# A pad that sets the distance of the normalised parts to the weights modulo 512 bytes, and decay matrices from plain broadcasts

## The chip, the core and the metric

The kernel runs on one core of one Trainium2 chip. The metric is the device time of one execution in microseconds (us): the median of three runs, and beside it one profiled execution whose trace all rows here come from. TensorE (PE) multiplies matrices, with a queue for loading weights beside it (PEld); VectorE (DVE) and ScalarE (ACT) work on whole tiles; GpSimd (POOL) and SyncE (SP) mostly issue transfers. The 16 DMA engines are shared by all queues.

## What is computed

Two layers of a hybrid backbone over 256 latent and 256 context tokens of width 1024, in float32. A layer has a SwiGLU half-step, a mixer, and a second half-step; each begins with a modulated RMS norm `n`. The mixer projects `n` once and runs two branches, of which this change touches the gated DeltaNet:

```
h += 1/2 * gate1 * SwiGLU(mod(RMSNorm(h)))
n  = mod(RMSNorm(h)); p = n @ W_in
  g = -exp(a_log) * softplus(p_ab + dt_bias);  g = cumsum(g) in a chunk
  decay = exp(where(i >= j, g_i - g_j, -inf))            # per token block, direction and head
  a_mat = (k beta) k^T * decay;  qk = q k^T * decay; ...
h += gate2 * (m @ W_out)
h += 1/2 * gate3 * SwiGLU(mod(RMSNorm(h)))
```

## The kernel before

**Products.** Every dense product is float32 split in two float32r parts: a weights tile of 1024 x 128 is loaded on SP's queue into `raw` (three buffers, 512 KB), ACT copies it to `whi` (L112) and DVE makes `wlo = raw - whi` (L113), three buffers each. `mm3` (L142) then makes three matmuls for each of the eight row blocks: whi x high part, whi x low part, wlo x high part of the activations. A projection is 24 matmuls of 512 columns (both token streams), or 2 x 24 of 256 where the streams are taken apart (`project_halves`, the first three columns of a stage), or 24 of 256 where only the latent stream is needed.

**Stages.** Six times `open_norm` allocates the pair `nh`, `nl` (each 8 x 512 floats a partition) on the right side of SBUF, and a stage of projections reads it: (1) the first half-step of layer 0, 44 projections, from 26 to 295 us in the profile; (2) its mixer, 65 projections, to 845; (3) its second half-step, 44, to 1328; (4) the first half-step of layer 1, 44, 1457 to 1709; (5) its mixer, mostly 256 columns, 1834 to 2139; (6) its last half-step, all 256 columns, 2315 to 2441. Between them stand the second products of the half-steps, which read `gh`, `gl`, and the mixer's others, which read `yh`, `yl`, `oh`, `ol`, `mh`, `ml`.

**Addresses.** In the built program every buffer of `whi` and `wlo` starts at 192 modulo 512 bytes, and each matmul's block of weights is 512 bytes wide, each row block of activations 2048. `nh` and `nl` start at 480 in all six stages, 288 behind the weights; so do `yh` and `yl`. `gh`, `gl`, `oh`, `ol`, `mh` and `ml` are at 192, distance 0.

**Decays.** `mixer` advances the generator of `decays` and `decay_matrices` by one step for each of its first projections. `decays` makes the cumulated log decays `gc` (tile `x` in the rows) and stores them as rows in DRAM (`grow`). `decay_matrices` fills R, two tiles of 2 directions x 2 blocks x 8 heads x 128 x 128. For each of the eight (stream, direction, block) it writes mask minus `gc` of its own position with DVE (L507), adds the row of all 128 positions by an accumulating transfer of 512 KB on POOL's queue (L511), and exponentiates 128x1024 on ACT (L513).

**Order.** The order on each engine is made by a scheduler when the program is built, from program order and priorities: the split of weights has high priority, and the depthwise conv (`cy`, L822 and L824, 8 x 31 taps a layer on DVE) fills in from the end of the decays. An engine runs its instructions in that order, so what stands behind a waiting one waits too.

Of the kernel before, what the change touches and what calls it, by code (L numbers as in the profile page):

```python
# [12 lines left out]
F32 = mybir.dt.float32  # L13
F32R = mybir.dt.float32r
AF = mybir.ActivationFunctionType
ALU = mybir.AluOpType
# [16 lines left out]
CP = (1000, 0)  # L33


def blk(b):
    return slice(32 * b, 32 * b + 32)

# [8 lines left out]
class Net:  # L47
# [3 lines left out]
    def __init__(self, ctx, tc, a, out):  # L51
        self.tc, self.nc, self.a, self.out = tc, tc.nc, a, out
        nc = tc.nc
        pool = lambda name, bufs, **kw: ctx.enter_context(tc.tile_pool(name=name, bufs=bufs, **kw))
        self.cp = pool("cp", 1)
        self.vp = pool("vp", 2)
        self.sp = pool("sp", 2)
        self.rawp = pool("rawp", 3)
        self.wp = pool("wp", 3)
        self.hp = pool("hp", 1)  # L60
        self.wk = pool("wk", 2)
        self.pm = pool("pm", 4, space=PSUM)
        self.px = pool("px", 4, space=PSUM)
        self.dp = pool("dp", 1, space=DRAM)
        self.beside([], 1)
        self.small = nc.sync
        cst = lambda name, n=128: self.cp.tile([128, n], F32, name=name)
        self.ident = cst("ident")
        make_identity(nc, self.ident)
        self.ones = cst("ones")  # L70
        nc.vector.memset(self.ones, 1.0)
        self.mhalf = cst("mhalf", 16)
        nc.vector.memset(self.mhalf, -0.5)
        self.tri = [cst("tri0"), cst("tri1")]
        make_upper_triangular(nc, self.tri[0])
        make_lower_triangular(nc, self.tri[1])
        self.cap = [cst("cap0"), cst("cap1")]
        for d in range(2):
            nc.vector.tensor_scalar(out=self.cap[d], in0=self.tri[d], scalar1=-1.0, scalar2=1e6, op0=ALU.add, op1=ALU.mult)
        self.sel = cst("sel", 63)  # L80
        nc.vector.memset(self.sel, 0.0)
        nc.vector.memset(self.sel[:, 31:32], 1.0)
# [274 lines left out]
    def open_norm(self):  # L357

        self.np_ctx = ExitStack()
        pool = self.np_ctx.enter_context(self.right("np"))  # L360
        self.n = (pool.tile([128, KT, T], F32R, name="nh"), pool.tile([128, KT, T], F32R, name="nl"))

    def norm(self, y, q, s, bc=None, ks=range(KT)):

        nc = self.nc
        nh, nl = self.n
        st = STREAM[s]
        bc = bc if bc is not None else self.rstd(self.acc[s], D)[:, :256]
        for k in ks:
            t1 = self.wk.tile([128, 256], F32, tag="t1", name="t1", bufs=3)  # L370
            nc.vector.scalar_tensor_tensor(out=t1, in0=self.h[:, k, st], scalar=y.nA[:, q, k, s:s + 1], in1=bc,  # L371
                                           op0=ALU.mult, op1=ALU.mult)
            B = y.mods[:, 3 * q, k, s:s + 1]
            nc.scalar.activation(out=nh[:, k, st], in_=t1, func=AF.Identity, bias=B)  # L374
            nc.vector.scalar_tensor_tensor(out=nl[:, k, st], in0=t1, scalar=B, in1=nh[:, k, st].bitcast(F32),  # L375
                                           op0=ALU.add, op1=ALU.subtract)
# [74 lines left out]
    def decays(self, y, ps):  # L451


        nc, sp = self.nc, self.sp
        flat = lambda x: x.rearrange("p d t h -> p (d t h)")
        ab = self.w512("ab")
        nc.vector.tensor_copy(out=ab[:32, :], in_=ps[:32, :])
        pt = self.psx()
        for t in range(4):
            nc.tensor.transpose(pt[:, t * 32:(t + 1) * 32], ab[:32, t * 128:(t + 1) * 128], self.ident[:32, :32])  # L460
        pv = pt[:, :128].rearrange("p (t x d h) -> p x d t h", t=4, x=2, d=2)
        x, g, e = self.cols("x"), self.cols("g"), self.cols("e")
        y.beta = self.cols("beta")
        nc.vector.tensor_tensor(out=x, in0=pv[:, 0], in1=self.dtb[:, y.l].unsqueeze(2).to_broadcast([128, 2, 4, 8]), op=ALU.add)
        for d in range(2):
            nc.scalar.activation(out=y.beta[:, d], in_=pv[:, 1, d], func=AF.Tanh, scale=0.5)
        nc.vector.tensor_scalar(out=flat(y.beta), in0=flat(y.beta), scalar1=0.5, scalar2=0.5, op0=ALU.mult, op1=ALU.add)

        nc.vector.scalar_tensor_tensor(out=flat(e), in0=flat(x), scalar=-1.0, in1=flat(x), op0=ALU.mult, op1=ALU.min)
        nc.scalar.activation(out=flat(e), in_=flat(e), func=AF.Exp)  # L470
        nc.scalar.activation(out=flat(e), in_=flat(e), func=AF.Ln, bias=self.ones[:, 0:1])
        nc.vector.scalar_tensor_tensor(out=flat(x), in0=flat(x), scalar=0.0, in1=flat(e), op0=ALU.max, op1=ALU.add)
        nc.vector.tensor_tensor(out=g, in0=x, in1=self.decay[:, y.l].unsqueeze(2).to_broadcast([128, 2, 4, 8]), op=ALU.mult)
        yield
        pg = self.psx()
        for d in range(2):
            nc.tensor.matmul(pg[:, d * 32:(d + 1) * 32], lhsT=self.tri[d], rhs=flat(g)[:, d * 32:(d + 1) * 32], start=True, stop=True)
        nc.tensor.matmul(pg[:, 64:128], lhsT=self.ones, rhs=flat(g), start=True, stop=True)
        y.gc = gc = x
        gl, y.egc, y.egl, y.kd = e, self.cols("egc"), self.cols("egl"), self.cols("kd")  # L480
        nc.vector.tensor_copy(out=flat(gc), in_=pg[:, :64])
        nc.vector.tensor_copy(out=flat(gl), in_=pg[:, 64:128])
        nc.scalar.activation(out=flat(y.egc), in_=flat(gc), func=AF.Exp)
        nc.scalar.activation(out=flat(y.egl), in_=flat(gl), func=AF.Exp)
        nc.vector.tensor_tensor(out=flat(gl), in0=flat(gl), in1=flat(gc), op=ALU.subtract)
        nc.scalar.activation(out=flat(y.kd), in_=flat(gl), func=AF.Exp)

        yield
        y.rows = []
        for j, v in enumerate((gc, y.egc)):  # L490
            ps = self.psx()
            nc.tensor.transpose(ps[:64, :128], flat(v), self.ident)
            sb = self.w512("gr")[:64, :128]
            nc.vector.tensor_copy(out=sb, in_=ps[:64, :128])
            dr = self.dp.tile([64, 128], F32, name=f"grow{y.l}{j}")
            nc.sync.dma_start(out=dr, in_=sb)
            y.rows.append(dr)

    def decay_matrices(self, y, R):

        nc = self.nc
        for s in range(2):
            for d in range(2):
                for tt in range(2):
                    t = 2 * s + tt
                    e = R[s][:, d, tt]
                    nc.vector.tensor_tensor(out=e, in0=self.cap[d].unsqueeze(1).to_broadcast([128, 8, 128]),  # L507
                                            in1=y.gc[:, d, t].unsqueeze(2).to_broadcast([128, 8, 128]), op=ALU.subtract)
                    r0 = d * 32 + t * 8
                    ev = e.rearrange("p h i -> p (h i)")  # L510
                    nc.gpsimd.dma_start(out=ev, in_=y.rows[0][r0:r0 + 8, :].rearrange("a b -> (a b)").partition_broadcast(128),  # L511
                                        accum_op=ALU.add)
                    nc.scalar.activation(out=ev, in_=ev, func=AF.Exp)  # L513
                    yield

    def inverse_norms(self, y, ss):
# [63 lines left out]
    def solve(self, y, R, pool):  # L580
# [8 lines left out]
        for s in range(2):  # L589
            for b in range(4):  # L590
                for d in range(2):
                    nc.scalar.activation(out=G[blk(b), d, s * 16:(s + 1) * 16, :],
                                         in_=R[s][blk(b), d, :, :, blk(b)].rearrange("p t h i -> p (t h) i"), func=AF.Copy)
# [23 lines left out]
    def merge_blocks(self, y, R, X, XT, pool, xpool, beside):  # L617
# [3 lines left out]
        XN = xpool.tile([128, 32, 64], F32, name="XN")  # L621
        XB = xpool.tile([128, 2, 32, 32], F32, name="XB")
        nc.gpsimd.memset(XN[blk(0), :, 32:], 0.0)
        nc.gpsimd.memset(XN[blk(3), :, :32], 0.0)
        for d in range(2):
# [510 lines left out]
```

## Time and profile before

| | us |
|---|---|
| median of 3 runs | 2510.61 (2509.51 to 2510.81) |
| profiled execution | 2517.16 |
| its span, first to last instruction | 2515.4 |
| PE busy in the span | 2410.1 (96%) |
| DVE busy | 1774.5 (71%) |
| ACT busy | 956.0 (38%) |

The three matmul groups on `nh` and `nl` and the three on `gh` and `gl` hold nearly all of PE's time. A matmul's duration in the trace runs from its start to the end of its results, so consecutive ones overlap, and their sum is more than the engine's busy time; what a matmul costs is the distance from its start to that of the next. PE's clock is at its full 2.4 GHz, shown as 1.0, but for short stretches behind idle time, where it is 0.5. The mixers hold the idle pieces: around 485 and 1890, where the decays are made, and later around the solve and the scan.

### The profile page before, as it was taken

How to read it: one execution, taken by the hardware profiler on the slowest of the kernel's cores; microseconds unless marked ns; L12 is line 12 of the kernel's file. 1: busy time of each engine (PE TensorE's matmuls, PEld its weight loads, DVE VectorE, ACT ScalarE, POOL GpSimd, SP SyncE). 2: the span in 40 equal slices, each digit the busy share in tenths (PEclk: the TensorE clock that was granted, in tenths of full speed). 3: DMA queues.
4: the chain of work that ended last, by engine and by line, in shares of the span. 5: the costliest groups of instructions: out<-in, count | busy, mean ns of one | idle time of the engine just before them, and what ended most of it. 6: DMA issues, size and time to landing. Idle time of an engine off the chain costs nothing. (4 is left out here: it accounts for less than half of the span.)

```text
span 2515.4 us, 38318 instructions
## 1 busy us (share of the span) xinstructions
PE 2410.1 (96%) x15099; PEld 2043.3 (81%) x15099; DVE 1774.5 (71%) x3023; ACT 956.0 (38%) x1578; POOL 51.7 (2%) x111
## 2 busy tenths in 40 slices
PE   7999999999999999999999999999988998978998
PEld 5777778787887887887777888778887886878998
DVE  4766777699999665576667564444468999966554
ACT  3222222435443643332222232222245556544443
POOL 0000000100000000000000000000010000000000
PEclk9999999999999999999999999999999999988999
DMA  8556665744644474455555544444466572355664
GB/s 253 165 164 175 173 176 172 170 133 113 207 137 118 145 224 151 116 156 158 163 157 160 152 126 126 126 125 133 120 173 178 169 218 79 108 174 164 198 184 138
DMA packets 566773, 394.61 MB, mean 157 GB/s; under 512 B 27704, under 2 KB 513218, under 8 KB 564930
## 3 DMA queue, kind: packets, MB, share of 16 engines
q1 hardware_dynamic: 555606, 371.33, 51.2%
q0 software_dynamic: 2304, 8.39, 1.7%
q10 hardware_dynamic: 8684, 12.45, 1.5%
q8 instruction: 118, 1.93, 0.3%
q14 instruction: 61, 0.50, 0.1%
HBM read 358.43 MB, written 33.69 MB: 156 GB/s over the span
## 5 line engine op out<-in xcount | busy, mean ns | idle before, releaser
L142 PE MATMUL pm<-nh,whi 128*128 128x512 f32 (+1 forms) x2544 | 907.8, 359 | 23.2 <-ACT whi L112 16.3
L142 PE MATMUL pm<-nh,wlo 128*128 128x512 f32 (+1 forms) x2544 | 903.3, 356 | 2.9 <-DVE wlo L113 2.2
L142 PE MATMUL pm<-nl,whi 128*128 128x512 f32 (+1 forms) x2544 | 903.3, 356 | 0.0
L112 ACT ACTIVATE whi<-raw 128x1024 fp32r<-128x1024 f32 (+1 forms) x450 | 469.1, 1044 | 1109.3 <-PE pm L142 857.7
L113 DVE TENSOR_TENSOR wlo<-raw,whi 128x1024 fp32r<-128x1024 f32 (+1 forms) x450 | 541.1, 1204 | 237.3 <-ACT whi L112 233.2
L142 PEld LDWEIGHTS pm<-nh,whi 128*128 128x128 f32 x2544 | 480.9, 190 | 115.1 <-ACT whi L112 25.1
L142 PEld LDWEIGHTS pm<-nh,wlo 128*128 128x128 f32 x2544 | 480.9, 189 | 79.2 <-DVE wlo L113 4.4
L142 PEld LDWEIGHTS pm<-nl,whi 128*128 128x128 f32 x2544 | 481.3, 190 | 73.6 <-DVE nl L375 1.0
L296 DVE SCALAR_TENSOR_TENSOR aacc<-adaw,sc,aacc 128x512 f32<-128x512 f32 x448 | 312.3, 747 | 164.8 <-DMA adaw<-ada_w_in 164.7
L824 DVE SCALAR_TENSOR_TENSOR cy<-cx,cdw,cy 128x512 f32<-128x512 f32 (+1 forms) x480 | 272.0, 612 | 1.3
L142 PE MATMUL pm<-gh,whi 128*128 128x512 f32 (+1 forms) x770 | 268.8, 349 | 1.7 <-DVE h L380 1.7
L142 PE MATMUL pm<-gl,whi 128*128 128x512 f32 (+1 forms) x770 | 267.4, 347 | 0.0
L142 PE MATMUL pm<-gh,wlo 128*128 128x512 f32 (+1 forms) x770 | 267.3, 347 | 0.0
L142 PEld LDWEIGHTS pm<-gh,whi 128*128 128x128 f32 x770 | 145.7, 189 | 26.4 <-issue 3.4
L142 PEld LDWEIGHTS pm<-gh,wlo 128*128 128x128 f32 x770 | 145.7, 189 | 18.9 <-issue 0.8
L142 PEld LDWEIGHTS pm<-gl,whi 128*128 128x128 f32 x770 | 145.7, 189 | 17.6
L428 DVE TENSOR_TENSOR silu<-silu,pm 128x512 f32<-128x512 f32 (+1 forms) x88 | 54.5, 619 | 77.3 <-PE pm L142 70.2
L380 DVE SCALAR_TENSOR_TENSOR h<-pm,gate,h 128x256 f32<-128x256 f32 x80 | 36.4, 480 | 63.3 <-PE pm L142 63.0
L112 ACT ACTIVATE gh<-silu 128x512 fp32r<-128x512 f32 (+1 forms) x88 | 50.5, 573 | 39.1 <-DVE silu L428 39.0
L374 ACT ACTIVATE nh<-t,mods 128x256 fp32r<-128x256 f32 x88 | 39.9, 502 | 61.1 <-DVE t L371 61.0
L113 DVE TENSOR_TENSOR gl<-silu,gh 128x512 fp32r<-128x512 f32 (+1 forms) x88 | 54.4, 618 | 0.0
L142 PE MATMUL pm<-mh,whi 128*128 128x256 f32 (+1 forms) x152 | 48.3, 320 | 2.2 <-ACT mh L112 2.2
(248 smaller groups left out, 2376.9 us busy)
## 6 DMA issues: line engine op xcount, KB each, us to landing
raw<-ffn_w_in SPq DMA_DIRECT2D x208, 512.0 KB, 4.1
adaw<-ada_w_in SPq DMA_DIRECT2D x144, 512.0 KB, 4.0
raw<-w_in_in SPq DMA_DIRECT2D x130, 512.0 KB, 4.2
raw<-ffn_w_in SPq DMA_DIRECT2D x64, 448.0 KB, 4.3
R<-grow POOLq DMA_DIRECT2D x16, 512.0 KB, 13.9
raw<-conv_proj_in SPq DMA_DIRECT2D x16, 512.0 KB, 6.5
raw<-dn_proj_in SPq DMA_DIRECT2D x16, 512.0 KB
raw<-w_out_in SPq DMA_DIRECT2D x16, 512.0 KB, 4.1
```

What stands on the lines that cost most here:

```text
L112: nc.scalar.activation(out=hi, in_=x, func=AF.Copy)
L113: nc.vector.tensor_tensor(out=lo, in0=x, in1=hi.bitcast(F32), op=ALU.subtract)
L142: nc.tensor.matmul(ps, lhsT=u[:, j, :], rhs=v[:, k, tok], start=k == 0 and p == 0, stop=k == n - 1 and p == 2)
L296: nc.vector.scalar_tensor_tensor(out=st.acc[:, s], in0=wt[:, j], scalar=c, in1=st.acc[:, s], op0=ALU.mult, op1=ALU.add)
L374: nc.scalar.activation(out=nh[:, k, st], in_=t1, func=AF.Identity, bias=B)
L380: self.nc.vector.scalar_tensor_tensor(out=self.h[:, m, st], in0=ps[:, st], scalar=y.gate[:, q, m, s:s + 1], in1=self.h[:, m, st], op0=ALU. ...
L428: nc.vector.tensor_tensor(out=t, in0=t, in1=pb[:, tok], op=ALU.mult)
L824: nc.vector.scalar_tensor_tensor(out=dst, in0=src, scalar=w, in1=dst, op0=ALU.mult, op1=ALU.add)
```

## The change

Two things are changed. `open_norm` allocates a third tile `home` behind the pair, used by nothing, whose size puts the pair at 0, 64, 256, 448, 288 and 288 bytes behind the weights modulo 512 in the six stages (starts at 192, 256, 448, 128, 480 and 480). And `decay_matrices` no longer accumulates: four plain broadcasts a layer of 1 MB each put the rows into R, DVE adds the mask, and the subtraction of `gc` moves into the exponential as its bias, one 128x128 instruction a head, with `ngc = -gc` made in `decays`.

```diff
+HOMES = (0, 64, 256, 448, 288, 288)
...
         self.n = (pool.tile([128, KT, T], F32R, name="nh"), pool.tile([128, KT, T], F32R, name="nl"))
+        pool.tile([128, ((288 - next(self.homes) - 32) % 512 + 32) // 4], F32, name="home")
...
             y.rows.append(dr)
+        y.ngc = self.cols("r")
+        nc.vector.tensor_scalar(out=flat(y.ngc), in0=flat(gc), scalar1=-1.0, scalar2=None, op0=ALU.mult)
 
     def decay_matrices(self, y, R):
...
+        for s in range(2):
+            for d in range(2):
+                r0 = d * 32 + s * 16
+                nc.gpsimd.dma_start(out=R[s][:, d].rearrange("p t h i -> p (t h i)"),
+                                    in_=y.rows[0][r0:r0 + 16, :].rearrange("a b -> (a b)").partition_broadcast(128))
         for s in range(2):
             for d in range(2):
                 for tt in range(2):
                     t = 2 * s + tt
                     e = R[s][:, d, tt]
-                    nc.vector.tensor_tensor(out=e, in0=self.cap[d].unsqueeze(1).to_broadcast([128, 8, 128]),
-                                            in1=y.gc[:, d, t].unsqueeze(2).to_broadcast([128, 8, 128]), op=ALU.subtract)
-                    r0 = d * 32 + t * 8
-                    ev = e.rearrange("p h i -> p (h i)")
-                    nc.gpsimd.dma_start(out=ev, in_=y.rows[0][r0:r0 + 8, :].rearrange("a b -> (a b)").partition_broadcast(128),
-                                        accum_op=ALU.add)
-                    nc.scalar.activation(out=ev, in_=ev, func=AF.Exp)
+                    nc.vector.tensor_tensor(out=e, in0=e, in1=self.cap[d].unsqueeze(1).to_broadcast([128, 8, 128]), op=ALU.add)
+                    for h in range(8):
+                        nc.scalar.activation(out=e[:, h], in_=e[:, h], func=AF.Exp, bias=y.ngc[:, d, t, h:h + 1])
                     yield
```

The scheduler orders the mixers anew; outside them the order stays. On DVE in the mixer of layer 0, from the first instruction on R (R_3394 and R_3395 are the two tiles, cap the masks, x is gc, cy the conv's taps), it was:

```order
L507 TENSOR_TENSOR R_3394<-cap_101,x 128x1024
L113 TENSOR_TENSOR wlo<-raw,whi 128x1024
L485 TENSOR_TENSOR e<-e,x 128x64
L507 TENSOR_TENSOR R_3394<-cap_101,x 128x1024
L507 TENSOR_TENSOR R_3394<-cap_102,x 128x1024 x2
L923 SCALAR_TENSOR_TENSOR glu<-glu,pm 128x512
L113 TENSOR_TENSOR wlo<-raw,whi 128x1024
L494 COPY gr<-px 64x128 x2
L507 TENSOR_TENSOR R_3395<-cap_101,x 128x1024 x2
L507 TENSOR_TENSOR R_3395<-cap_102,x 128x1024 x2
L113 TENSOR_TENSOR wlo<-raw,whi 128x1024
```

The same place in the changed kernel, from behind the copies of the rows (R_3396 and R_3397 are the two tiles):

```order
L833 SCALAR_TENSOR_TENSOR cy<-cx,cdw,cy 128x512 x5
L117 TENSOR_TENSOR wlo<-raw,whi 128x1024
L833 SCALAR_TENSOR_TENSOR cy<-cx,cdw,cy 128x512 x3
L831 TENSOR_SCALAR cy<-cx,cdw,v_209 128x512
L833 SCALAR_TENSOR_TENSOR cy<-cx,cdw,cy 128x512 x2
L520 TENSOR_TENSOR R_3396<-R_3396,cap_101 128x1024
L117 TENSOR_TENSOR wlo<-raw,whi 128x1024
L932 SCALAR_TENSOR_TENSOR glu<-glu,pm 128x512
L520 TENSOR_TENSOR R_3396<-R_3396,cap_101 128x1024
L520 TENSOR_TENSOR R_3396<-R_3396,cap_102 128x1024 x2
L117 TENSOR_TENSOR wlo<-raw,whi 128x1024
```

The eight instructions on R stood ahead of the transfers and now stand behind them, with taps of the conv and the copies of the rows (`gr`) ahead of them. On ACT in the mixer of layer 1, around the first exponentials (R_14856 is R's first tile), it was:

```order
L112 ACTIVATE whi<-raw 128x1024
L513 ACTIVATE R_14856<-R_14856 128x1024
L112 ACTIVATE whi<-raw 128x1024
L513 ACTIVATE R_14856<-R_14856 128x1024
L922 ACTIVATE glu<-pm 128x256
L513 ACTIVATE R_14856<-R_14856 128x1024
L112 ACTIVATE whi<-raw 128x1024
```

And in the changed kernel (R_14915 is that tile, r is ngc):

```order
L116 ACTIVATE whi<-raw 128x1024 x2
L931 ACTIVATE glu<-pm 128x256
L522 ACTIVATE R_14915<-R_14915,r 128x128 x6
L116 ACTIVATE whi<-raw 128x1024
L522 ACTIVATE R_14915<-R_14915,r 128x128 x7
L116 ACTIVATE whi<-raw 128x1024
L522 ACTIVATE R_14915<-R_14915,r 128x128 x6
```

One whi more stands ahead of the first exponential, and from there on five to seven exponentials of 128x128 stand between two whi, where one or two of 128x1024 stood.

## Rows read from the trace of the kernel before

**Rows 1.** The page's engines, and the span with the granted clock of TensorE.

```profile
PE 2410.1 (96%) x15099; PEld 2043.3 (81%) x15099; DVE 1774.5 (71%) x3023; ACT 956.0 (38%) x1578; POOL 51.7 (2%) x111
...
core 0: 2515.4 us, clock 0.984
```

**Rows 2.** Groups by shape: count, busy us, mean ns of one, idle before.

```profile
L142 PE MATMUL pm<-nl,whi 128*128 128x512 f32 x1632 | 647.0, 397 | 0.0
...
L142 PE MATMUL pm<-nl,whi 128*128 128x256 f32 x912 | 256.4, 284 | 0.0
...
L142 PE MATMUL pm<-gl,whi 128*128 128x512 f32 x462 | 180.3, 390 | 0.0
```

**Rows 3.** Line 142: count, ns min/median/max, first and last start; two stretches.

```profile
L142 PE MATMUL pm<-nl,whi x158: 393/395/397, 1584.8 to 1694.7; 128*128 128x512 f32 x158
...
L142 PE MATMUL pm<-gh,wlo x119: 389/389/389, 1714.7 to 1794.9; 128*128 128x512 f32 x119
```

**Rows 4.** The same at 256 columns, in three stretches.

```profile
L142 PE MATMUL pm<-nl,whi x315: 277/278/280, 2324.8 to 2434.7; 128*128 128x256 f32 x158
...
L142 PE MATMUL pm<-ml,whi x26: 283/283/283, 1050.8 to 1059.8; 128*128 128x256 f32 x26
...
L142 PE MATMUL pm<-yh,whi x40: 280/280/280, 2256.0 to 2269.7; 128*128 128x256 f32 x40
```

**Rows 5.** Stretches: width; busy (count) of PE, PEld, DVE, ACT, POOL; clock, DMA.

```profile
26.00:295.00 269.00, 266.08 (x1284) 206.93 (x1281) 186.52 (x286) 80.47 (x111) 0.00 (x0) 1.00 0.63 179
520.00:640.00 120.00, 119.70 (x522) 91.97 (x521) 119.54 (x167) 53.85 (x105) 1.36 (x16) 1.00 0.47 136
1070.00:1328.00 258.00, 256.21 (x1193) 204.79 (x1192) 175.92 (x264) 77.86 (x105) 1.07 (x1) 1.00 0.55 157
```

**Rows 6.** Stretches beside the decays of the two mixers.

```profile
463.00:498.00 35.00, 30.00 (x126) 22.89 (x124) 20.00 (x27) 14.65 (x16) 7.90 (x8) 0.99 0.91 198
498.00:501.00 3.00, 3.00 (x7) 2.42 (x8) 3.00 (x5) 1.06 (x2) 0.00 (x0) 0.51 0.59 150
1866.00:1900.40 34.40, 21.19 (x144) 20.08 (x142) 15.35 (x21) 14.25 (x16) 7.03 (x8) 0.80 1.00 214
1883.00:1887.00 4.00, 4.00 (x22) 3.94 (x21) 0.85 (x1) 1.99 (x2) 0.86 (x1) 0.57 1.07 215
1895.70:1900.40 4.70, 4.16 (x18) 3.87 (x18) 4.65 (x10) 4.70 (x7) 0.00 (x0) 0.50 0.67 171
```

**Rows 7.** Waits (us, times, longest) from 463 and from 1866; one row of PE's timeline.

```profile
ACT R L513 <- DMA R<-grow: 18.1, 6, 8.4
...
PE pm L142 <- ACT whi L112: 11.8, 2, 8.6
ACT whi L112 <- DMA raw<-w_in_in: 7.5, 1, 7.5
...
1881.51 0.39 PE L142 MATMUL pm<-nh,whi 128*128 128x256 f32 x1 [3.18 <-ACT whi L112]
```

**Rows 8.** DMA queues (packets, MB, share): from 468:493, 1874:1892, 930:936.

```profile
q0 software_dynamic: 1149, 4.19, 85.1%
...
q0 software_dynamic: 918, 3.37, 94.1%
q1 hardware_dynamic: 915, 0.47, 12.6%
...
q1 hardware_dynamic: 622, 2.39, 97.9%
```

**Rows 9.** Instructions on R, and others like the new exponentials, on DVE and ACT.

```profile
L507 DVE TENSOR_TENSOR R<-cap,x x16: 1206/1216/1219, 452.1 to 1882.6; 128x1024 f32<-128x1024 f32 x16
...
L112 ACT ACTIVATE whi<-raw 128x1024 fp32r<-128x1024 f32 x13 | 13.7, 1053 | 15.3 <-DMA raw<-w_in_in 7.5 <-PE pm L142 5.2 <-issue 2.5
L513 ACT ACTIVATE R<-R 128x1024 f32<-128x1024 f32 x8 | 8.3, 1054 | 12.0 <-DMA R<-grow 12.0
...
L878 ACT ACTIVATE osq<-o x48: 292/294/354, 881.8 to 2218.8; 128x128 f32<-128x128 f32 x48
```

More of the change, by code (lines that the diff above doesn't have):

```diff
@@ L66, in __init__ @@
         self.small = nc.sync
+        self.homes = iter(HOMES)
         cst = lambda name, n=128: self.cp.tile([128, n], F32, name=name)
```

## The prediction

> **What bounds the kernel now.** I read the page's engine line first [rows 1]: TensorE (PE) is busy 96% of the span at a mean granted clock of 0.984, so time goes where PE matmuls go, or where PE waits. The groups by shape come next [rows 2]: 1632 × 3 matmuls of 512 columns and 912 × 3 of 256 columns read nh or nl, 462 × 3 of 512 columns read gh or gl. Their mean durations (397, 390 ns) overlap and are no price; the price is the distance from one start to the next. For that I took stretches in which PE runs one shape without a break and divided first to last start by the count. In [rows 3], nl,whi x158 starts from 1584.8 to 1694.7: 109.9 us over 157 × 3 steps, as three groups alternate, is 233.3 ns a matmul. gh,wlo x119 from 1714.7 to 1794.9 is 80.2 over 118 × 3, 226.6 ns. Same shape, same weights tiles, same full clock. What differs is the address: nh and nl start 288 bytes behind the weights modulo 512, gh and gl at 0. At 256 columns it is the other way round [rows 4]: nl x315, 109.9 over 314 × 3, 116.7 ns; ml (distance 0) x26, 9.0 over 25 × 3, 120.0 ns. The durations say the same without a division: 389 ns at every matmul of gh against 393 to 397, 283 for ml against 277 to 280 for nl and 280 for yh, which also stands at 288. So the distance matters, by 6.7 ns one way and 3.3 the other.
>
> Here the Trainium skill speaks against the change. "TensorE: Matmul & The Clock Gate", section "Step-by-step: what each phase is for", says that PE has two independent SBUF read ports, so that loading the next weights doesn't steal read bandwidth from the running matmul. By that rule the pad would change nothing, and the sum would keep its second half alone. The two starts above disagree with it, and it is weighed as a rival below.
>
> Last I looked for PE's idle time. The largest single pieces lie where each mixer makes its decays [rows 6]: in 463 to 498 PE is busy 30.0 of 35.0, and the next 3.0 run at clock 0.51; in 1866 to 1900.4 PE is busy 21.19 of 34.4, and of that two pieces of 4.0 and 4.16 run at 0.57 and 0.50.
>
> **Part A, the pad.** It adds no instruction. Distances become 0, 64, 256, 448, 288, 288 in the order of the stages: first half-step of layer 0, its mixer, its second half-step, first half-step of layer 1, its mixer, last half-step. The last two stay as they are. Counts follow from the loops, 24 matmuls a projection:
> - Stage 1: 44 projections, 1056 matmuls of 512 columns, distance 0, the one row I have. About 1000 of them lie in unbroken runs: 1000 × 6.7 = 6.7 us.
> - Stages 3 and 4: 41 projections in 512 columns, 984 each, and 3 in halves, 144 of 256. With the price of distance 0 each gives 984 × 6.7 = 6.6, less 144 × 3.3 = 0.5: 6.1 us, together 12.2.
> - Stage 2: 62 projections, 1488 × 6.7 = 10.0, less 0.5. Here VectorE (DVE) is the cover that could run out: 119.54 of 120 us busy in 520 to 640 [rows 5], with the depthwise conv between the splits. The order of its instructions is fixed, so a PE that is 2.9% faster leads to a wait for wlo once the lead of three weight buffers is used up. DVE is busy only 20.00 of the 35 us beside the decays [rows 6], and gets some of that back. I take 7.5 us of the 9.5.
>
> In stages 1 and 3 DVE is busy 186.52 of 269 and 175.92 of 258 [rows 5], and stage 4 has stage 3's products, so nothing is late next there.
>
> No row shows 64, 256 or 448. The rows bound them by 0 (as at 288) and 6.7 ns (as at 0). 256 is only 32 from 288, which speaks for nothing; but 0, 64, 256 and 448 are whole multiples of 64 and 288 is not, and 64 and 448 are 64 from 0. I take 6.7 for all three and keep the ends. Below the lower end: a distance may also be as much worse than 288 as 0 is better, 240 ns. Above: 512 columns at 2.4 GHz are 213.3, 13.2 ns more than the row at 0 leaves.
> Sum of part A: 6.7 + 12.2 + 7.5 = 26.4 us; ends of it 6.7 and, with another 6.7 ns on 3456 matmuls, 49.
>
> **Part B, the decays.** Removed, per layer: 8 accumulating transfers of 512 KB on POOL's queue, 8 DVE subtractions of 1.22 us, 8 exponentials of 1.05 us [rows 9]. Added: 4 plain broadcasts of 1 MB, 8 DVE additions of the same shape (1.22, no difference), one 128x64 negation (a sixteenth of the columns), 64 exponentials of 128x128. What the old transfers cost is in [rows 8]: in layer 0 they move 4.19 MB in the 25 us from 468; in layer 1, from 1874 to 1892, they hold 94.1% of the 16 DMA engines and move 3.37 MB in 18 us, 187 GB/s, while the queue of the weights gets 0.47 MB, less than one 512 KB tile. That is what PE waits for [rows 7]: PE for whi 11.8 us, whi for raw 7.5, and [rows 9] the exponentials for their transfers 12.0, with whi behind them on ScalarE (ACT). Loss now: layer 0, 5.0 idle + 3.0 × 0.5 at half clock = 6.5; layer 1, 13.2 idle + 1.7 + 2.1 at half clock = 17.0.
>
> A plain transfer in large packets reaches 2.39 MB in 6 us, 400 GB/s [rows 8]; 4.19 MB take 10.5 us alone, some 12 beside the weights, against 25. In layer 1 the hold begins at 1866, and PE's first wait of more than a microsecond at 1878.3 (a start at 1881.51 after 3.18 idle, [rows 7]): PE went on for 12 us on what was in buffers. So the new hold ends about when PE runs dry; one tile must then land and be split, about 4 us of idle time, with one dip of the clock (1.7). In layer 0 a projection takes twice as long, the buffers last twice as long, and I leave 1 us.
>
> The new cost is on ACT. A 128x128 exponential lies between an eighth of the old one, 0.13, and the longest osq, 0.35 (a Square of 128x128, SBUF to SBUF) [rows 9]; it has osq's shape, so I take osq's 0.294. 64 × 0.294 = 18.8 us a layer against 8 × 1.05 = 8.4. The waiting instruction's followers are whi and glu on ACT: in layer 1 six exponentials (1.8) stand between two whi (1.05), 2.8 us and what glu takes, some 3.0 a projection where PE needs 24 × 0.1167 = 2.8. Over ten projections 2 us. New waits: the DVE addition waits for the broadcast, with wlo queued behind it; since the conv's taps and several wlo now stand ahead of the first addition, I price it at 0, at most the 8.4 us that ACT's longest wait for a transfer lasts now [rows 7]. Left after: layer 0 1, layer 1 4 + 1.7 + 2 = 7.7. Gain 5.5 + 9.3 = 14.8, taken as 15. Ends: 23.5 (all of it), and 0 (ACT's 2 × 10.4 us take it back).
>
> **Sum.** The profiled execution took 2517.2 us, 1.8 around its span of 2515.4. Less 26.4 and 15 it is 2475.8. The median of the runs is 2510.6, 6.6 below the profiled one; less 41.4 it is 2469.
>
> **The rivals.**
> - *Only some distances help.* One or more of 64, 256, 448 behaves as 288. For: 288 itself is an unlucky one, with 256 beside it. Losing stages 2 to 4 leaves 6.7 + 15 = 22: 2489. Chance 18%.
> - *The distances are better than 0.* Another 6.7 ns on 3456: 2469 − 20 = 2449. Nothing in the rows excludes it. Chance 13%.
> - *The pad does nothing:* nl and gl differ by something other than the address. Against: yh, in another tile, has durations like nl's, and ml, again in another, is slower than both [rows 4]. Only part B: 2510.6 − 15 = 2496. Chance 5%. This is also what the Trainium skill's rule above would lead to.
> - *The broadcasts do nothing.* Packets twice as large starve the weights as before, or ACT is the bound. Only part A: 2484. Chance 12%.
> - *The distances are worse: slower than before.* Place: stages 2 to 4, 3456 matmuls of 512 columns. At 240 ns they cost 23 us more, against 7 from stage 1, and with ACT's longer exponentials eating part B, 2510.6 + 16 = 2527. With part B kept it decides from 239.6 ns on average, (6.7 + 15) / 3456 = 6.3 above 233.3; with part B gone from 235.2. Chance 5%.
>
> **How the numbers follow.** The forecast, all four distances about like 0 and the decays mostly free, has the rest, 47%, and gives 2469 ± 14. The range goes from 2440 (better distances with most of the 23.5) to 2500 (part B alone, or half of both). About 0.2%, 5 us, is what a measurement can tell from no change: faster than 2505.6 has 91%, as the only cases that reach it are the last one and a failure of both parts (4%); slower 5%.
>
> **What would show it.** Right: the 512-column step in stage 1 falls to 226.6 and the durations to 389 throughout; the steps of stages 2 to 4 lie at or below that; the last two stages keep 116.7; in the decays' stretch of each mixer the software queue's hold falls from 25 to 12 us, PE's waits for whi from 11.8 to about 4. Wrong: steps of 233 or more at 64, 256 or 448; PE waiting for wlo from 520 to 800 with DVE full; ACT full between the exponentials with PE waiting for whi.

## The result, and the profile after

The changed kernel takes 2482.33 us in the median of four runs (2477.48 to 2488.85) beside 2510.45 us for the kernel before: a ratio of 0.989, 95% interval 0.9867 to 0.9913. The prediction was 2469 us, in a range of 2440 to 2500. The sign and the range held; 28 us came where 41.4 were forecast.

The page's engines and the span of the profiled execution after, which answer to [rows 1]:

```profile
PE 2391.7 (96%) x15099; PEld 2048.7 (82%) x15099; DVE 1775.8 (71%) x3025; ACT 976.6 (39%) x1690; POOL 41.0 (2%) x103
...
core 0: 2487.0 us, clock 0.983
```

TensorE (PE) is busy 18.4 us less, and ScalarE (ACT) 20.6 us more, which are the exponentials in pieces; VectorE (DVE) is where it was, 1775.8 for 1774.5. The gain is placed by the stages. The table gives each stage's length in us, from its first matmul on `nh` or `nl` to the first matmul of what follows (on `gh` behind the projections of a half-step, on `yh` in the mixer of layer 0, on `oh` in that of layer 1), for five profiled executions (the last three columns belong to experiments below):

| stage (distance after) | before | after | pad only | broadcasts only | best distances |
|---|---|---|---|---|---|
| 1, first half-step, layer 0 (0) | 268.0 | 262.1 | 262.2 | 266.7 | 261.2 |
| 2, mixer, layer 0 (64) | 453.0 | 441.5 | 449.8 | 446.7 | 441.1 |
| 3, second half-step, layer 0 (256) | 257.5 | 251.8 | 251.2 | 255.7 | 251.0 |
| 4, first half-step, layer 1 (448) | 252.1 | 251.7 | 251.7 | 252.0 | 246.0 |
| 5, mixer, layer 1 (288) | 389.1 | 385.4 | 388.0 | 383.3 | 381.4 |
| 6, last half-step (288) | 125.8 | 125.9 | 126.0 | 126.7 | 121.8 |

Stages 1 and 3 became 5.9 and 5.7 us shorter, close to the forecast (6.7 and 6.1). Stage 4 became 0.4 shorter where 6.1 were forecast. Single lengths are good to about 2 us: with the broadcasts alone, which leave stages 1 and 3 as they are, these are 1.3 and 1.8 us shorter. The steps say why. Line 146 of the kernel after is the line of [rows 3] (count, ns min/median/max of a duration, first and last start in us); one stretch each of stages 1 to 4, then the halves of stage 4 at 256 columns:

```profile
L146 PE MATMUL pm<-nh,whi x70: 387/390/396, 222.3 to 269.3; 128*128 128x512 f32 x70
...
L146 PE MATMUL pm<-nl,whi x144: 391/392/393, 450.7 to 548.9; 128*128 128x512 f32 x144
...
L146 PE MATMUL pm<-nh,whi x78: 387/389/396, 1181.8 to 1234.2; 128*128 128x512 f32 x78
...
L146 PE MATMUL pm<-nh,whi x166: 392/396/399, 1554.8 to 1670.3; 128*128 128x512 f32 x166
...
L146 PE MATMUL pm<-nh,whi x32: 275/276/367, 1440.0 to 1450.6; 128*128 128x256 f32 x32
```

First to last start, divided by three times the count less one, is 227.0, 228.9, 226.8 and 233.3 ns at distances 0, 64, 256 and 448, where [rows 3] have 233.3 at 288. So 256 is as good as 0, 64 gives two thirds of it, and 448 gives nothing at 512 columns. At 256 columns 448 gives 10.6 / 93 = 114 ns, less than any row before had (116.7 and 120.0, [rows 4]).

In the decays of layer 0 PE no longer stops. Stretches as in [rows 6] (width, then busy of PE, PEld, DVE, ACT, POOL, then clock, DMA share, GB/s), the third of the decays of layer 1, the last one of the rest of that mixer; then PE's and ACT's waits from 1836 to 1880 and a row of SyncE's timeline (start, us, instruction):

```profile
455.00:490.00 35.00, 35.00 (x155) 28.75 (x154) 31.91 (x41) 23.31 (x64) 2.33 (x4) 1.00 0.74 244
490.00:493.00 3.00, 3.00 (x15) 2.47 (x14) 3.00 (x5) 3.00 (x12) 0.00 (x0) 1.00 0.28 101
1841.00:1875.40 34.40, 27.77 (x212) 27.07 (x211) 23.95 (x31) 21.35 (x55) 2.17 (x4) 0.90 0.84 267
2064.00:2109.00 45.00, 38.14 (x736) 31.43 (x723) 37.97 (x79) 26.16 (x42) 0.45 (x4) 0.81 0.25 71
```

```profile
ACT whi L116 <- DMA raw<-w_in_in: 8.3, 1, 8.3
...
PE pm L146 <- ACT whi L116: 6.1, 1, 6.1
```

```profile
1844.16 9.95 SPq L123 DMA_DIRECT2D raw<-w_in_in  x2
```

Against [rows 6], layer 0 has PE busy for 35.0 of 35.0 at full clock (30.0 before), layer 1 for 27.77 of 34.4 at clock 0.90 (21.19 at 0.80). One wait of 6.1 us is left in layer 1, for a tile that ACT got 8.3 us late: SyncE asked for it while POOL's queue was full. The plain broadcasts themselves are as forecast. DMA queues from 1842 to 1855, against [rows 8]:

```profile
q0 software_dynamic: 569, 4.15, 79.5%
q1 hardware_dynamic: 1482, 0.64, 18.9%
```

4.15 MB in 13 us, where 12 were forecast and the accumulating transfers took 25 in layer 0 and moved 187 GB/s in layer 1.

### The profile page after: what moved, and what is told of

The parts are those of the page before. It is cut to its first block, busy times and chain, and to the rows that moved or that the text cites. A ratio compares the mean times of both kernels' runs of the same rounds, so it can differ in the third digit from the quotient of the medians.

```text
span 2487.0 us, 38426 instructions
## 1 busy us (share of the span) xinstructions
PE 2391.7 (96%) x15099; PEld 2048.7 (82%) x15099; DVE 1775.8 (71%) x3025; ACT 976.6 (39%) x1690; POOL 41.0 (2%) x103
## 6 DMA issues: line engine op xcount, KB each, us to landing
R<-grow POOLq DMA_DIRECT2D x8, 1024.0 KB, 10.1
```

## The experiments

Numbers of single executions here are read by their stretches, because the total also contains what the clock gives: the mean granted clock of whole executions of the same kernel was 0.983 (after) and 0.989 (repeat of it).

**One part alone, twice.** The first kernel keeps the pad and goes back to accumulating decays; the second keeps the broadcasts and puts every stage at 288.

```diff
 # pad only: decay_matrices and decays as in the kernel before
-                nc.gpsimd.dma_start(out=R[s][:, d]..., in_=y.rows[0][r0:r0 + 16, :]...partition_broadcast(128))
+                    nc.gpsimd.dma_start(out=ev, in_=y.rows[0][r0:r0 + 8, :]..., accum_op=ALU.add)
 # broadcasts only
-HOMES = (0, 64, 256, 448, 288, 288)
+HOMES = (288, 288, 288, 288, 288, 288)
```

> The pad with its distances 0, 64, 256, 448, 288, 288, and the decays by accumulating transfers as before. Theory (the step of a matmul depends on the distance alone, the two parts add): stage 1 loses 6.6 us, stage 2 1488 x (233.3 - 228.9) = 6.5 less 0.2 for its 144 matmuls of 256 columns, stage 3 5.7, stage 4 0.4: 19 us, so about 2491. Rival (in stage 2 VectorE is full, and only the broadcasts freed it, so the parts need one another): stage 2 gains less than 3 of its 6.3, and the time is 2495 or more.

> Plain broadcasts, with the normalised parts at 288 in all six stages. Theory (parts add): the mixer of layer 0 gains 11.6 - 6.3 = 5.3 us, that of layer 1 4.9, of which the scan gives back about 1: 9 us, so about 2501. Rival (the pad is what gained in the mixer of layer 0, or ScalarE's 64 exponentials a layer eat it): under 4 us, 2507 or more.

Measured: pad only 2497.98 us in the median (ratio 0.9957, 0.9941 to 0.9972), broadcasts only 2498.17 (0.9952, 0.9935 to 0.997); before 2509.64 on that chip. So 11.7 and 11.5 us. Their sum of 23.2 and the 28.1 of both agree within the intervals, but stage 2 doesn't add: the pad alone gained 3.2 us there, the broadcasts alone 6.3, both 11.5. Comparing the start of every 96th matmul with the kernel before shows where. With the broadcasts under it the pad gains 0.4 us at each 96 matmuls of 512 columns, which would be 1488 × 4.4 ns = 6.5 us; it loses 0.8 of that where PE waits once for DVE (`ssb`, L531), and 5.2 are left at the end (441.5 for 446.7). Without them the first 0.6 us are kept, but at the decays nothing is added, and a later wait takes 1.5 back. PE's and ACT's waits in the decays of layer 0 (455 to 500) with the pad alone, and PE's in the kernel before (463 to 498):

```profile
ACT R L518 <- DMA R<-grow: 18.2, 6, 8.6
...
PE pm L146 <- ACT whi L116: 4.6, 2, 2.6
```

```profile
PE pm L142 <- ACT whi L112: 3.9, 2, 2.5
```

A PE that comes 0.6 us earlier waits that much longer for transfers whose length hasn't changed. The theory that the parts simply add is a little off, and the rival (under 3 us in stage 2, 2495 or more) comes nearer for this kernel. For the broadcasts alone the theory holds by the stages (6.3 us for 5.3 in layer 0, 5.8 for some 4 in layer 1). The decays themselves gained more, 7.4 us in layer 0 and 9.8 in layer 1 by the same comparison, and lost part of it again before the stage's end; in layer 0 PE waits 4.0 us in the solve (its matmuls on `XT` and `Y`, near 760 us) for 2.2 before.

**Two sweeps of the distance.**

```diff
-HOMES = (0, 64, 256, 448, 288, 288)
+HOMES = (32, 96, 128, 160, 192, 224)      # first sweep
+HOMES = (320, 352, 384, 416, 480, 32)     # second sweep
```

> The changed kernel with distances 32, 96, 128, 160, 192, 224: six more points of the step. Theory A (a smooth course that rises with the distance at 512 columns and falls at 256): between 0 (226.9, 119.9) and 288 (233.3, 116.7) the step at 512 columns rises and that at 256 falls. Theory B (what counts is the distance modulo 256, since 0 and 256 agree): 32 is as 288 (233.3 at 512 columns, 116.7 at 256), 192 as 448 (233.3 and 113.5 or lower).

> The changed kernel with distances 320, 352, 384, 416, 480, 32: the other half of the table. Theory (the step repeats every 256 bytes, as 32 and 288, 0 and 256, 192 and 448 agree where they were seen): 320 as 64 (about 229 ns at 512 columns), 352 as 96 (231 to 237; 120 at 256 columns), 384 as 128 (231.5; 119), 416 as 160 (234; 118), 32 as 288 (116.7 at 256 columns). Rival (period of 512 bytes): 320 and 352 lie on the course from 288 to 448, 233.3 both, and 113.5 to 116.7 at 256 columns.

Line 146 in long stretches: first sweep at 32 and 160, and at 192 (256 columns); second sweep at 320 and 416:

```profile
L146 PE MATMUL pm<-nh,whi x70: 392/394/397, 226.4 to 274.7; 128*128 128x512 f32 x70
...
L146 PE MATMUL pm<-nh,whi x144: 391/397/401, 1464.8 to 1565.3; 128*128 128x512 f32 x144
...
L146 PE MATMUL pm<-nh,whi x120: 276/276/279, 2009.7 to 2050.2; 128*128 128x256 f32 x120
```

```profile
L146 PE MATMUL pm<-nh,wlo x70: 394/394/477, 222.7 to 270.1; 128*128 128x512 f32 x70
...
L146 PE MATMUL pm<-nh,whi x144: 392/397/400, 1460.8 to 1561.3; 128*128 128x512 f32 x144
```

They are 233.3 at 32, 234.3 at 160, 113.4 at 192, 229.0 at 320, 234.3 at 416. The two kernels took 2505.04 and 2493.52 us, one run each. All distances together, as steps in ns within unbroken stretches:

| distance modulo 256 | 512 columns | 256 columns |
|---|---|---|
| 0 (0, 256) | 226.8 | 119.9 |
| 32 (32, 288) | 233.3 | 116.7 (117.8 in some) |
| 64 (64, 320) | 228.9 | 117.8 |
| 96 (96, 352) | 233.3 | 119.9 |
| 128 (128, 384) | 232.3 to 233.3 | 118.7 |
| 160 (160, 416) | 234.3 | 117.3 |
| 192 (192, 448) | 233.3 | 113.4 (117.8 in some) |
| 224 (224, 480) | 233.3 | 118.3 |

Each pair agrees wherever both were seen (64 and 320 only at 512 columns, 224 and 480 only at 256), so the step repeats every 256 bytes; theory B of the first sweep and the theory of the second hold, and the smooth courses fall. At 512 columns only 0 and 64 are clearly better than 288; at 256 columns only 192 is.

**The distance or the address.** Everything on the left side of SBUF, the weights with it, moves by 128 bytes, and the pads move the normalised parts as far.

```diff
+        pool("shift", 1).tile([128, 32], F32, name="shift")
         self.rawp = pool("rawp", 3)
-HOMES = (0, 64, 256, 448, 288, 288)
+HOMES = (128, 192, 384, 64, 416, 416)     # distances 0, 64, 256, 448, 288, 288
```

> The changed kernel with everything on the left side of SBUF, the weights among it, shifted by 128 bytes, and the pads set so that all distances stay as in the changed kernel. Theory (the distance counts): steps of 226.9, 228.9, 226.8 and 233.3 ns in stages 1 to 4 at 512 columns, 113.5 in stage 4's halves, 116.7 in stage 6, as in the changed kernel. Rival (the address of the normalised parts itself counts): they now start at 320, 384, 64, 256, 96 and 96 modulo 512, where 320 and 384 took 231.5 and 234 ns in the last sweep, and stage 1 goes to 231.5.

Line 147 of that kernel in stages 1 and 4:

```profile
L147 PE MATMUL pm<-nh,whi x70: 389/389/393, 221.6 to 268.6; 128*128 128x512 f32 x70
...
L147 PE MATMUL pm<-nh,wlo x166: 394/394/399, 1548.8 to 1664.3; 128*128 128x512 f32 x166
```

47.0 / 207 = 227.1 and 115.5 / 495 = 233.3; stage 2 has 228.9, stage 3 226.8, stage 4's halves 113.7, stage 6 116.7, all as in the changed kernel (2484.12 us, one run). `yh` stays where it was while the weights move, and so comes to 160: its step at 256 columns is 117.3 in place of 117.8, which is the table's value for 160. The distance counts, not the address.

**The best distances.** Made after the first result, from its own steps.

```diff
-HOMES = (0, 64, 256, 448, 288, 288)
+HOMES = (0, 0, 256, 0, 448, 448)
```

> The changed kernel with distances 0, 0, 256, 0, 448, 448. Theory (steps go by the distance): at 512 columns 226.9 ns in stages 1 to 4, at 256 columns 113.5 in stages 5 and 6 and 119.9 in the halves of stages 2 to 4. Against the changed kernel stage 2 gains 1488 x 2.0 - 144 x 2.1 = 2.7 us, stage 4 984 x 6.4 - 144 x 6.4 = 5.4, stages 5 and 6 some 1250 and 1056 x 3.2 = 4.0 and 3.4: 15.5 us, so about 2467. Rival (the step belongs to the stage and what runs beside it, not to the distance): stage 4 stays at 233.3 and stages 5 and 6 at 116.7, 2480. Rival (weights can't come faster in stages 5 and 6): 2474.

Measured 2469.22 us (2468.87 to 2473.28), ratio 0.9844 (0.9826 to 0.9862): 13 us below the changed kernel, and below its interval. Line 146 in stages 4 and 6, then in two stretches of stage 5:

```profile
L146 PE MATMUL pm<-nh,wlo x166: 387/389/396, 1547.1 to 1659.4; 128*128 128x512 f32 x166
...
L146 PE MATMUL pm<-nl,whi x346: 276/276/278, 2274.9 to 2391.9; 128*128 128x256 f32 x173
...
L146 PE MATMUL pm<-nh,whi x39: 276/276/307, 1854.8 to 1867.7; 128*128 128x256 f32 x39
...
L146 PE MATMUL pm<-nh,whi x119: 281/281/282, 1984.7 to 2026.4; 128*128 128x256 f32 x119
```

Stage 4 has 226.9 now and gains 5.7 us, stage 6 has 113.3 (over all starts of the three groups) and gains 4.1: the distance theory. Stage 2 kept 0.4 of the 2.7 us expected: it was 1.5 ahead at its 1345th matmul on `nh` and `nl`, and lost that in the solve behind it (734.6 to 770.4), where its mean granted clock is 0.90 for 0.95 in the changed kernel (737.8 to 772.2). Stage 5 is 4.0 us shorter in the table, as expected, but not for the reason expected: by its 1537th matmul, of 1632, it had gained 1.0, and the rest came where the clock differs between the two executions (0.88 for 0.81, see below). At the same 448 it runs at 113.4 ns in some stretches and at 117.8 in others, as the last two rows show by their durations. Within an unbroken run of matmuls the value stays, and it changes from one run to the next: in this trace all of 1854.9 to 1868.3 has the short step, all of 1984.5 to 2026.7 the long one. What sets it at the start of a run isn't settled.

**What is left in the decays of layer 1.** Three edits of the broadcasts. Half the packet size, same queue:

```diff
+                for tt in range(2):
-                nc.gpsimd.dma_start(out=R[s][:, d]..., in_=y.rows[0][r0:r0 + 16, :]...)
+                    nc.gpsimd.dma_start(out=R[s][:, d, tt]..., in_=y.rows[0][r0:r0 + 8, :]...)
```

> The changed kernel with eight plain broadcasts of 512 KB a layer for four of 1 MB, so 4 KB packets for 8 KB ones. Theory (a queue's turn is one packet, so the size of the broadcast's packet sets what the weights get): the weights get twice as much while it lasts, 4.19 x 512 / 4096 = 0.52 MB for 0.26, PE's wait for the split in the mixer of layer 1 falls from 6.1 us by about half a tile's time to 4 to 5, with a hold of 12 to 13 us. Rival (the hold's length alone sets it): 6.1 as it is.

Queues of the changed kernel from 1846 to 1854, and of this one from 1842 to 1850:

```profile
q0 software_dynamic: 394, 2.94, 90.0%
q1 hardware_dynamic: 414, 0.21, 10.7%
```

```profile
q0 software_dynamic: 765, 2.79, 85.7%
q1 hardware_dynamic: 780, 0.45, 17.9%
```

In both the two queues move nearly equal numbers of packets, and with packets of half the size the weights get twice the bytes, 0.45 MB for 0.21. The Trainium skill says the same in "DMA: Bandwidth & Descriptors", section "Queues, rings and completion order": a DMA engine goes round its queues packet by packet. Yet PE's wait grew, from 6.1 to 7.1 us (the kernel took 2476.32 us, one run, at a mean clock of 0.989). Its timeline and two rows of ACT's:

```profile
1855.58 0.58 PE L146 MATMUL pm<-nh,whi 128*128 128x256 f32 x1 [7.08 <-ACT glu L932]
```

```profile
1853.62 1.06 ACT L116 ACTIVATE whi<-raw 128x1024 fp32r<-128x1024 f32 x1 [1.60 <-DMA raw<-w_in_in]
...
1855.17 0.36 ACT L932 ACTIVATE glu<-pm 128x256 f32<-128x256 f32 x1
```

The first late tile was split at 1848.92 (1858.32 in the changed kernel), but PE waited for a result tile `pm` that `glu` reads, and `glu` stood in ACT's order behind nine exponentials and the next `whi`, which waited for its own tile. So the share of the weights was as the theory said, and its price wasn't: another wait took the place.

Next, the broadcasts as eight on SP's queue, between the loads of the weights:

```diff
+        def fetch():                       # the next of the eight blocks (s, d, tt)
+            if todo:
+                s, d, tt = todo.pop(0)
+                nc.sync.dma_start(out=R[s][:, d, tt]..., in_=y.rows[0][r0:r0 + 8, :]...)
+        fetch()
...
                     e = R[s][:, d, tt]
+                    fetch()
```

> The changed kernel with the broadcasts as eight of 512 KB on SP's queue, between the loads of the weights, in place of four of 1 MB on POOL's queue. Theory (what costs in the mixer of layer 1 is that a second queue starves the weights for as long as it is full): each broadcast delays the weights by 1.3 us, five in a row by 6.5, which the three buffers cover; no wait of PE over 3 us there, and the mixer of layer 1 falls from 385.4 by about 6 to 379, that of layer 0 stays: about 2476. Rival (the bytes have to pass either way, and a load behind them waits the same): a gap of 6 us at another place, 2482.

Measured 2485.12 us (2481.62 to 2489.71; ratio 0.9901, 0.9882 to 0.992): no better than the changed kernel. Its waits in the decays of layer 1 (1842 to 1886):

```profile
ACT whi L116 <- DMA raw<-w_in_in: 3.2, 4, 1.4
...
PE pm L146 <- ACT whi L116: 1.9, 1, 1.9
...
PE pm L146 <- DVE wlo L117: 1.1, 1, 1.1
```

The mechanism holds: 6.1 us of waiting became 1.9 + 1.1, and the matmuls behind the decays come 4.9 us earlier against the stage's start. But the mixer of layer 0, whose order the scheduler changed too, is 6.1 us longer (447.6 for 441.5), in three pieces well behind the decays. So a third kernel has the best distances, POOL's broadcasts in layer 0, and SP's in layer 1 only, and ran beside the changed kernel once more:

```diff
-HOMES = (0, 64, 256, 448, 288, 288)
+HOMES = (0, 0, 256, 0, 448, 448)
...
+        # layer 0: four broadcasts on POOL's queue; layer 1: fetch() as above
```

> Distances 0, 0, 256, 0, 448, 448, the broadcasts of layer 0 on POOL's queue as in the changed kernel, those of layer 1 as eight on SP's queue between the loads of the weights. Theory (the two add): 2469.2 less the 4.9 us that the decays of layer 1 gained by the paced broadcasts, about 2464.5. Rival (the products of layer 1 after the projections, which wait for other engines, give it back): 2468 to 2470.

> The changed kernel itself once more, for a comparison on one chip with the two others. Its four runs lay between 2477.5 and 2488.9. Theory (the spread is what the clock loses behind idle pieces, and runs to either side): 2482 within 3. Rival (the profiled run was the odd one): 2478.

Measured on another chip, on which the kernel before took 2513.79 us, some 4 us more: 2475.37 us (2466.03 to 2482.87), ratio 0.9844 (0.9822 to 0.9867), and 2486.36 (2484.59 to 2490.84) for the changed kernel, ratio 0.9895 (0.9879 to 0.9911). The changed kernel is 4.4 us above its theory and its ratio is as before (0.989). The third kernel is 10.9 us above its theory and 5 above its rival. As ratios to the kernel before on the first chip the theory is 0.982 and the rival 0.983 to 0.984. The third kernel, at 0.9844, is where the best distances alone were, so the rival holds. Its decays in layer 1 gained 3.9 us against the best distances, and of that 2.1 were left at the end of stage 5 (379.3 for 381.4).

**Are the exponentials in the way?**

```diff
-                    for h in range(8):
-                        nc.scalar.activation(out=e[:, h], in_=e[:, h], func=AF.Exp, bias=y.ngc[:, d, t, h:h + 1])
+                    nc.scalar.activation(out=ev, in_=ev, func=AF.Exp)
```

> The changed kernel with one exponential of 128x1024 for each eight of 128x128, as the kernel before had; it leaves out the subtraction of a position's own cumulated decay. Theory (ScalarE's 64 exponentials a layer lie beside other work, and the weights' transfers make the wait): in the mixer of layer 1 PE's wait for the split stays at 6.1 us within 0.5, and the matmuls after the decays are at most 2 us earlier against the stage's start; in layer 0 nothing. Rival (ScalarE's queue makes the wait): it falls below 4 us, and the mixer of layer 1 gains more than 2.

One run on the second chip, 2490.61 us: PE's wait in layer 1 is 5.3 us, beside 5.2 in the changed kernel on that chip; the matmuls behind the decays come 0.9 us later than there, and layer 0 has the same length (440.1 for 440.4). The theory holds: eight exponentials for one cost nothing that can be seen.

## Why the prediction was right, and where it was off

**The bound and the mechanism: right.** PE's matmuls set the time, and their step depends on the distance of the two operands. The Trainium skill's two independent read ports ("TensorE: Matmul & The Clock Gate", section "Step-by-step: what each phase is for") would leave all steps alike; 226.8, 228.9, 233.3 and 234.3 ns for one shape at one clock say otherwise, and the shifted kernel shows that it is the distance.

**Stages 1 and 3: right.** 6.7 and 6.1 us forecast, 5.9 and 5.7 found.

**"I take 6.7 for all three": the step that failed.** The reason given was that 0, 64, 256 and 448 are multiples of 64. What the sweeps show is a period of 256 with no such rule: 256 gives 6.5 ns because it is 0, 64 gives 4.4, and 448, which is 192, gives nothing at 512 columns. One of the prediction's own signs of being wrong, steps of 233 or more at 448, came true. Stage 4 gained 0.4 us for 6.1, and that little comes from its 144 matmuls of 256 columns. Stage 2 gained 5.2 us by the pad for 7.5: 1488 × 4.4 = 6.5, and waits took 1.3 where 2 had been left out for DVE's cover (DVE is busy 119.02 of 120 us from 520 to 640, for 119.54 in [rows 5]). Part A is then 5.9 + 5.2 + 5.7 + 0.4 = 17.2 by the stages for 26.4: this is the rival that only some distances help, in a milder form. (The rival with better distances should have stood at 2446: 3456 × 6.7 ns is 23 us, not 20.)

**The decays, part B: right at the decays, and a third of it lost behind them.** At the decays layer 0 gained 7.4 us for 5.5: no wait was left there, where 1 us was allowed. Layer 1 gained 8.0 in the profiled execution and 10.1 in the repeat for 9.3. At the ends of the stages 6.3 and 3.7 are left, 10.0 us for 15; by the medians the broadcasts alone give 11.5. The hold of 12 us and the price of an exponential (2.14 us for seven, a whi 2.04 behind the first: 0.29) were as worked out. "One tile must then land and be split, about 4 us" was 6.1, since the tile had been asked for early in the hold and got one packet of 512 bytes for each of 8192. The 2 us for ACT were nothing, as the kernel with single exponentials shows.

**What nobody priced: the end of stage 5.** From its last 96 matmuls on `nh` and `nl` on, the changed kernel gave back 4.3 of its 8.0 us. None of its instructions there is new, but the scheduler has put some in another order. Its mean granted clock from 2064 to 2109 is 0.81. The kernel before in the same place, and the repeat of the changed kernel in its:

```profile
2097.00:2139.00 42.00, 34.12 (x718) 28.24 (x717) 38.31 (x81) 26.11 (x42) 0.46 (x4) 0.92 0.27 78
```

```profile
2060.00:2110.00 50.00, 40.88 (x889) 33.50 (x889) 45.61 (x92) 33.58 (x52) 0.46 (x4) 0.93 0.27 76
```

In this stretch PE stands idle three times for 2 to 3 us in each of the three executions, and behind that its clock is 1.2 instead of 2.4 GHz for a while: at 0.81 that is 38% of 45 us, at 0.92 16% of 42. The repeat, the same program on the second chip, kept the clock at 0.93, and its stage 5 took 377.0 us for 385.4. So the program alone doesn't bring the loss about. Whether the change has a part in it stays open: of the ten traces not taken on the second chip, the two with accumulating decays have 0.92 in this stretch, and the eight with plain broadcasts 0.81 to 0.88. The kernels with one part alone, the pad first:

```profile
2077.90:2119.70 41.80, 34.25 (x727) 28.40 (x716) 38.24 (x80) 26.22 (x42) 0.45 (x4) 0.92 0.27 76
```

```profile
2077.20:2122.50 45.30, 38.22 (x717) 31.44 (x716) 37.71 (x78) 26.02 (x42) 0.45 (x4) 0.81 0.25 70
```

The four runs of the changed kernel go with the clock as a whole: 2488.85 us at a mean clock of 0.983, 2482.09 at 0.984, 2482.57 at 0.986, 2477.48 at 0.987; that the clock makes most of their spread is a guess from that, not tested, and the third kernel has 2475.37 and 2482.87 us both at 0.983. By the stages, 17.2 + 6.3 + 3.7 − 0.1 (stage 6) = 27.1 us, against 28.4 between the two spans; the rest lies between the stages.

## What to carry to other kernels

Where matmuls with 32-bit operands follow each other without a gap, measure the distance from start to start for each tile that is read, and look at where the operands stand to each other modulo 256 bytes; the best distance depends on the number of columns (here 0 at 512, 192 at 256), so a pad is chosen per stage, from a sweep and not from a rule. A broadcast on a second queue is paid for by the queue beside it in packets, not in bytes: read from the trace when the load that PE needs next was asked for, not only how long the broadcast holds the engines. And a gain of a few microseconds in front of a stretch that waits for several engines was kept only in part here (3.7 of 8.0 us, 2.1 of 3.9), so it has to be read at the end of the stage.

## What the runs showed of the hardware

- The step of a matmul of 128x128 weights in float32r depends on the distance between its activations and the weights with a period of 256 bytes: 226.8 to 234.3 ns at 512 columns, 113.4 to 119.9 at 256. What is best for one width is not for the other.
- At some distances two values occur at 256 columns: 116.7 and 117.8 ns at 288, 113.4 and 117.8 at 192 and 448, for the same shape, tiles and clock. One value holds through an unbroken run (stage 6 at 288 has 116.7 throughout in the changed kernel, 117.8 throughout in that with the pad alone). So the distance alone doesn't fix it; what else does is open.
- Two DMA queues that are both full move nearly equal numbers of packets, whether they are 8192 bytes on one side (394 beside 414 of 512 bytes in 8 us) or 4096 (765 beside 780).
- On the second chip stage 1 was 3 to 5 us longer in all three kernels; near 150 us DVE waits 8.6 to 9.0 us for the `adaw` transfers there, for 5.7 in the changed kernel on the first. Times of different chips are compared here by their ratios to the kernel before.
